# Neighbour broadcast by stream shuffles, and transposes in other places, in a two-layer hybrid decoder trunk

## The chip, the cores and the metric

The kernel runs on one core of a Trainium2 chip. The metric is the device time of one execution in microseconds. PE is the matrix engine, DVE the vector engine, ACT the scalar engine, POOL the general-purpose engine; SP issues most DMAs. Before the change three runs took 1132.7 to 1134.36 us, with a median of 1132.71 us.

## The reference

Input `x` is 1 x 256 x 1024 in float32. There are two layers. Each adds half a SwiGLU feed-forward step, a mixer, and another half step, each on the RMS norm of `x`; a last RMS norm follows. The mixer is what the change is about:

```python
def hybrid_mixer(h, ...):
    proj = h @ w_in                      # 1024 x 7636: all inputs of the branches and the gates
    # a: indexer and sparse attention
    rel   = relu(einsum('bqhd,bsd->bqhs', q_idx, k_idx) * 64 ** -0.5)   # after partial rotary
    score = einsum('bqhs,bqh->bqs', rel, w_idx)
    _, sel = top_k(score, top_k)         # then attention over the selected keys
    # b: forgetting attention
    # c: gated delta rule, chunk 64, on convolved q, k, v (4 heads of 128)
    a_mat = where(strict, einsum('nbhid,nbhjd->nbhij', kb, kc) * decay, 0)
    sol = triangular_solve(a_mat + eye(64), rhs, lower=True, unit_diagonal=True)
    ...
    return (sum_i sigmoid(gate_i) * (y_i @ P_i)) @ w_out

def rms_norm(x, gain):
    return x * rsqrt(mean(x * x) + 1e-6) * gain
```

## The kernel before

**Weights.** All products with weights keep float32 accuracy by splitting both operands into a high and a low part. A weight comes in units of 128 x 2 x 512 (512 KB). SP loads a unit into one of four `raw` buffers; ACT copies it to the reduced type (`hi`) and DVE subtracts (`lo`), into one of three pairs of buffers. PE uses a unit in one of three forms: three products of 512 columns per block of 128 rows (`form_a`, with the tokens as output rows), or with the weight's rows as output (`form_b`), or products of 512 and 256 columns (`form_w`).

**Order.** `Emit` writes the program: while the products of the weight units are emitted, tasks (the branches, normalisations, the merge's halves) are advanced step by step when a modelled clock passes their due time (`E.tick`, `E.run`, `E.finish`). Then a scheduler with a model of the engines sets the order on each engine; splits of weights and evacuations of accumulators have a higher priority. Every engine runs its instructions in that order.

**A mixer** multiplies the normed input with the units of q, k, v of branch c, of the small projection (`sm`), of a's queries, z, b's q and k (`bqk`) and v, then the gates and branches in the order gate 0, gate 1, branch a, gate 2, branch b, branch c, and then `w_out`. Beside these products run the tasks:

- *Branch a* (`branch_a`): POOL rotates `sm` (`rope`) and copies the keys twice (`kdup`); PE transposes (tile `ti`, two tiles of four 128 x 128 transposes); ACT and DVE split the results into `akh`, `akl`, `iqs`. PE multiplies them to scores (`ix`), DVE sums over heads (`score`) and takes the top entries in rounds of MAX8 and MATCH_REPLACE8. The query side of the attention (`qs`) is split in the same way.
- *Branch c* (`branch_c`): of the 128 x 128 triangular matrices it takes the 16 x 16 blocks on the diagonal (`nd`, 8 of each kind in the 8 matrices), packs them into `cp16` (128 x 128) by a reduction, and inverts all by substitution in 15 steps of `ztmp` and `zc` on DVE. Step m needs row m of every block on all 16 partitions of the block. That is the neighbour broadcast: `cp16` is written to a DRAM tile `dr`, and two DMAs read it back into `nb`, each partition of a block getting the block's 16 rows (lines 631 to 635):

```python
dr = dp.tile([P, P], F32, name="dr", tag="dr")
nc.sync.dma_start(dr, cp16)
for i in range(2):
    nc.sync.dma_start(nb[i], bass.AP(tensor=dr.tensor, offset=dr.offset + i * 1024,
                                       ap=[[2048, 8], [0, 16], [1, 1024]]))
```

- *The gates* (`gate`): a product into two accumulator banks, evacuated by DVE with the bias (tile `gate`) and by ACT with tanh. The product after next needs those banks.
- *The merge* (`branch`, `m_half`): DVE multiplies each branch's product by its gate and adds it up in `mrg`. `m_half(n)` transposes half n of it (tile `mt`, 8 transposes) and splits it into pairs `mp` (ACT copies, DVE subtracts). It is a task; `E.finish(mt[u // 2])` completes half 0 ahead of unit 0 of `w_out` and half 1 ahead of unit 2.

**The norm** (`rms`, six times a run: at the start of each half step and mixer): the squares, summed over the feature blocks into `ssum`, are summed over the partitions by products with a column of ones (tile `ss`, 128 x 1, two products), scaled on DVE and raised to the power -1/2 on POOL (`rstd`).

## Time and profile before

| | |
|---|---|
| median of three runs | 1132.71 us |
| the profiled execution | 1133.0 us, of which its span 1131.2 us |
| mean granted PE clock | 0.996 |
| busy: PE, DVE, ACT, POOL | 1108.3, 842.2, 652.2, 198.0 us |
| chain that ended last | PE 91%, DVE 4%, DMA 2%, the rest 1% or less each |
| DMA | 194.07 MB, mean 172 GB/s |

A busy share of 98% says that PE is nearly always at work, and so the list of what stops it is short. Times inside the profile count from the span's start. The mixer of layer 1 begins its tasks near 140 us and ends its merge near 440 us; the second has the same stretches about 557 us later. [...]

### The profile page before, as it was taken

The numbers are of one execution on the slowest core, as the hardware profiler recorded it, in microseconds if no ns is written. First come the engines' busy times: TensorE is split into PE (matmuls) and PEld (weight loads), VectorE is DVE, ScalarE is ACT, GpSimd is POOL, SyncE is SP. The second block draws the span as 40 slices with busy tenths as digits, with TensorE's granted clock in tenths as the row PEclk, the third lists the DMA queues.
The fourth block names the chain that finished last, engine by engine and source line by source line (L and its number), as shares of the span: only waits on it lengthen the run. The fifth ranks groups of instructions, "written<-read, shape, count | busy, mean of one in ns | idle before, by whom it ended". The sixth has DMA issues, their size and how long they took to land.

```text
span 1131.2 us, 17844 instructions
## 1 busy us (share of the span) xinstructions
PE 1108.3 (98%) x6765; PEld 954.2 (84%) x6765; DVE 842.2 (74%) x1373; ACT 652.2 (58%) x1136; POOL 198.0 (18%) x172
## 2 busy tenths in 40 slices
PE   9999999998999999999999999999999999999997
PEld 7888898987778878888888889979877788888886
DVE  7776689879746677876678767888796658787753
ACT  6655455644758645655465645564647685556543
POOL 4322022100000203322032311040000003033210
PEclk9999999999999999999999999999999999999999
DMA  8665655555434354666556555555554344556652
GB/s 285 205 186 189 190 178 184 165 146 167 149 113 144 128 179 154 213 195 188 187 171 202 186 193 182 177 169 168 152 177 150 104 130 147 169 171 200 187 191 91
DMA packets 56375, 194.07 MB, mean 172 GB/s; under 512 B 6240, under 2 KB 8672, under 8 KB 56288
## 3 DMA queue, kind: packets, MB, share of 16 engines
q1 hardware_dynamic: 55856, 192.32, 53.2%
q8 instruction: 53, 0.87, 0.3%
q10 hardware_dynamic: 432, 0.60, 0.1%
q14 instruction: 34, 0.28, 0.1%
HBM read 191.72 MB, written 1.18 MB: 171 GB/s over the span
## 4 chain that ended last, share of the span: by engine, by line
PE 91%; DVE 4%; DMA 2%; issue 1%; POOL 1%; ACT 1%; POOLq 0%; DVEq 0%; ACTq 0%
PE pw L148 48%; PE pt L148 25%; PE pbr L148 6%; PE po L148 4%; DMA nb<-dr 2%; DVE lo L86 1%; PE lg L148 1%; PE pv L148 1%; PE pT L152 1%; PE lv L148 1%; PE lw L148 1%; DVE score L86 1%; PE gq L148 1%; DVE ztmp L86 0%; POOL rp L86 0%
## 5 line engine op out<-in xcount | busy, mean ns | idle before, releaser
L86 DVE TENSOR_TENSOR lo<-raw,hi 128x1024 fp32r<-128x1024 f32 (+2 forms) x353 | 451.2, 1280 | 178.8 <-ACT hi L86 178.2
L86 ACT ACTIVATE hi<-raw 128x1024 fp32r<-128x1024 f32 (+2 forms) x353 | 372.6, 1057 | 353.9 <-PE pw L148 155.7
L148 PE MATMUL pw<-xt,hi 128*128 128x512 f32 x1024 | 349.0, 396 | 0.8 <-ACT hi L86 0.8
L148 PE MATMUL pw<-xt,lo 128*128 128x256 f32 x1024 | 263.8, 280 | 0.0
L148 PEld LDWEIGHTS pw<-xt,hi 128*128 128x128 f32 x1024 | 189.3, 189 | 37.7 <-ACT hi L86 1.7
L148 PE MATMUL pt<-hi,xt 128*128 128x512 f32 (+1 forms) x640 | 206.5, 398 | 4.7 <-DVE gate L86 4.7
L148 PEld LDWEIGHTS pw<-xt,lo 128*128 128x128 f32 x1024 | 193.0, 189 | 9.0 <-DVE lo L86 0.7
L148 PEld LDWEIGHTS pt<-hi,xt 128*128 128x128 f32 x640 | 120.5, 191 | 28.7 <-issue 5.8
L148 PE MATMUL pw<-ht,hi 128*128 128x512 f32 x384 | 132.2, 394 | 0.0
L148 PE MATMUL pt<-lo,xt 128*128 128x512 f32 (+1 forms) x320 | 127.9, 400 | 1.7 <-DVE lo L86 1.7
L148 PE MATMUL pt<-xt,hi 128*128 128x256 f32 x640 | 118.1, 285 | 0.0
L148 PE MATMUL pw<-ht,lo 128*128 128x256 f32 x384 | 103.4, 279 | 0.0
L148 PEld LDWEIGHTS pt<-xt,hi 128*128 128x128 f32 x640 | 99.6, 191 | 0.2
L148 PE MATMUL pt<-xt,lo 128*128 128x256 f32 x320 | 89.7, 284 | 0.0
L148 PEld LDWEIGHTS pw<-ht,hi 128*128 128x128 f32 x384 | 71.4, 188 | 15.2
L86 POOL TENSOR_TENSOR hr<-hg,rbc 128x512 f32<-128x512 f32 x32 | 42.3, 1323 | 213.8 <-DVE hg L86 204.5
L148 PEld LDWEIGHTS pw<-ht,lo 128*128 128x128 f32 x384 | 72.4, 188 | 1.5
L148 PEld LDWEIGHTS pt<-lo,xt 128*128 128x128 f32 x320 | 61.0, 191 | 14.2 <-DVE lo L86 2.6
L86 POOL TENSOR_TENSOR hg<-hr,rbc 128x512 f32<-128x512 f32 x32 | 66.9, 2090 | 2.5
L86 POOL TENSOR_TENSOR ssum<-ssum,sq 128x512 f32<-128x512 f32 x18 | 28.6, 1588 | 199.3 <-ACT sq L86 199.3
L148 PEld LDWEIGHTS pt<-xt,lo 128*128 128x128 f32 x320 | 60.8, 191 | 0.0
L86 POOL TENSOR_TENSOR so<-so,mhalf 128x8 f32<-128x8 f32 x2 | 3.3, 1642 | 284.9 <-DVE so L86 284.9
(254 smaller groups left out, 1498.6 us busy)
## 6 DMA issues: line engine op xcount, KB each, us to landing
raw<-in_wmx SPq DMA_DIRECT2D x112, 512.0 KB, 3.7
raw<-in_wf2i SPq DMA_DIRECT2D x64, 512.0 KB, 3.8
raw<-in_wf1i SPq DMA_DIRECT2D x63, 512.0 KB, 4.2
raw<-in_wf1o SPq DMA_DIRECT2D x32, 512.0 KB, 4.2
raw<-in_wf2o SPq DMA_DIRECT2D x32, 512.0 KB, 4.2
raw<-in_wbr SPq DMA_DIRECT2D x24, 512.0 KB, 3.3
raw<-in_wmo SPq DMA_DIRECT2D x16, 512.0 KB, 4.1
raw<-in_wms SPq DMA_DIRECT2D x8, 468.0 KB, 3.8
```

The costliest lines, as they stand in the source:

```text
L86: return f(*args, **kw)
L148: self.nc.tensor.matmul(out, lhsT, rhs, start=start, stop=stop, skip_group_check=True)
L152: self.nc.tensor.transpose(out, in_, ident)
```

## The change

It has four parts.

1. In `branch_c` the DMAs to and from DRAM go. DVE makes the broadcast with 15 `stream_shuffle` instructions, which pick for each of 32 partitions the partition it reads: in shuffle m all 16 partitions of a block read partition m, and only the columns from m + 1 on are moved.
2. In `rms` the two products with ones become two transposes of 128 x 128, and DVE sums each over the free axis.
3. The index transposes `ti` are pinned by `tc.issue_after(E.pe.ins)`: they are not issued before the last product that has been emitted when the task's step is written.
4. The merge: half 0 is transposed between the two token blocks of the last unit of branch c (`mid`), half 1 ahead of the third row block of `w_out`'s unit 1 (`midway`), both pinned in the same way; the waits by `E.finish` go.

```diff
         return self.parts.pop(self.used - 1)
 
     def mm(self, out, lhsT, rhs, start=True, stop=True, cost=0.218):
-        self.nc.tensor.matmul(out, lhsT, rhs, start=start, stop=stop, skip_group_check=True)
+        self.pe = self.nc.tensor.matmul(out, lhsT, rhs, start=start, stop=stop, skip_group_check=True)
         self.t += cost
 
     def tr(self, out, in_, ident):
-        self.nc.tensor.transpose(out, in_, ident)
+        self.pe = self.nc.tensor.transpose(out, in_, ident)
         self.t += 0.11
 
     def add(self, gen, rank=0, pace=PACE):
...
     rawp = ctx.enter_context(tc.tile_pool(name="rawp", bufs=NR))
     hlp = ctx.enter_context(tc.tile_pool(name="hlp", bufs=NH))
     wk = ctx.enter_context(tc.tile_pool(name="wk", bufs=2))
-    dp = ctx.enter_context(tc.tile_pool(name="dp", bufs=2, space=bass.MemoryType.DRAM))
     ps = ctx.enter_context(tc.tile_pool(name="ps", bufs=4, space=bass.MemoryType.PSUM))
     pa = ctx.enter_context(tc.tile_pool(name="pa", bufs=2, space=bass.MemoryType.PSUM))
     pc = ctx.enter_context(tc.tile_pool(name="pc", bufs=2, space=bass.MemoryType.PSUM))
...
 
     def rms(st):
 
-        pt = pa.tile([P, 512], F32, name="ss", tag="s")
+        pt = pa.tile([P, 2, P], F32, name="ss", tag="s")
         for tb in range(2):
-            E.mm(pt[:, tb:tb + 1], st["sq"][:, tb * P:(tb + 1) * P], ones[:, 0:1], tb == 0, tb == 1, cost=0.11)
+            E.tr(pt[:, tb, :], st["sq"][:, tb * P:(tb + 1) * P], ident)
         r = st["r"] = wk.tile([P, 2], F32, name="rstd", tag="rstd", bufs=2)
-        V.tensor_scalar(r, pt[:, 0:2], 1.0 / D, EPS, op0=OP.mult, op1=OP.add)
+        V.tensor_reduce(r, pt, axis=AX.X, op=OP.add)
+        V.tensor_scalar(r, r, 1.0 / D, EPS, op0=OP.mult, op1=OP.add)
         G.tensor_tensor(out=r, in0=r, in1=mhalf[:, :2], op=OP.pow)
 
     def x_half(nrm, n, st, pt=None):
...
                 E.mm(o, wl[:, i, m0:m0 + P], xk(xt, 0, k), False, b, 0.109)
             E.tick()
 
-    def form_w(pt, xt, ks, wh, wl, first, last):
+    def form_w(pt, xt, ks, wh, wl, first, last, midway=None):
 
 
         for m in range(4):
             m0 = m * P
+            if m == 2 and midway is not None:
+                midway()
             for i in range(UK):
                 k = ks + i
                 E.mm(pt[m], wh[:, i, m0:m0 + P], xt[k // 2][:, k % 2], first and i == 0, False, 0.216)
...
         cp16 = tiny("cp16", P, 1)
         V.tensor_reduce(v3(cp16, 8), nd.rearrange("p (q k r) -> p q r k", q=8, k=8), axis=AX.X, op=OP.add)
         V.tensor_copy(v3(zc, 8), cst[:, None, C_E16:C_E16 + 16].to_broadcast([P, 8, 16]))
-        dr = dp.tile([P, P], F32, name="dr", tag="dr")
-        nc.sync.dma_start(dr, cp16)
-        for i in range(2):
-            nc.sync.dma_start(nb[i], bass.AP(tensor=dr.tensor, offset=dr.offset + i * 1024,
-                                               ap=[[2048, 8], [0, 16], [1, 1024]]))
+
+        nbv = [t.rearrange("p (m q r) -> p m q r", m=8, q=8) for t in nb]
+        for m in range(15):
+            nc.vector.stream_shuffle(nbv[m // 8][:, m % 8, :, m + 1:], v3(cp16, 8)[:, :, m + 1:],
+                                     [16 * (i // 16) + m for i in range(32)])
         yield
         rk = tiny("rk", 8)
         G.tensor_tensor(out=rk, in0=ssk, in1=phalf, op=OP.pow)
...
         tmp = tiny("ztmp", P, 1)
         for m in range(15):
             k = 15 - m
-            V.tensor_tensor(out=v3(tmp, 8)[:, :, :k], in0=nb[m // 8].rearrange("p (m q r) -> p m q r", m=8, q=8)[:, m % 8, :, m + 1:],
+            V.tensor_tensor(out=v3(tmp, 8)[:, :, :k], in0=nbv[m // 8][:, m % 8, :, m + 1:],
                             in1=zv[:, :, m:m + 1].to_broadcast([P, 8, k]), op=OP.mult)
             V.tensor_tensor(out=zv[:, :, m + 1:], in0=zv[:, :, m + 1:], in1=v3(tmp, 8)[:, :, :k], op=OP.subtract)
             if m % 4 == 3:
...
                 V.tensor_tensor(d[other], src[own], d[own].bitcast(F32), op=OP.subtract)
         for tb in range(2):
             pt = pa.tile([P, 4, P], F32, name="ti", tag="s")
-            for i in range(2):
-                E.tr(pt[:, i, :], sm[:, tb, S_IQ + i * P:S_IQ + (i + 1) * P], ident)
-                E.tr(pt[:, 2 + i, :], kdup[:, 256 * tb + 128 * i:256 * tb + 128 * (i + 1)], ident)
+            with tc.issue_after(E.pe.ins):
+                for i in range(2):
+                    E.tr(pt[:, i, :], sm[:, tb, S_IQ + i * P:S_IQ + (i + 1) * P], ident)
+                    E.tr(pt[:, 2 + i, :], kdup[:, 256 * tb + 128 * i:256 * tb + 128 * (i + 1)], ident)
             t0 = tb * P
             S.activation(kh[:, :, t0:t0 + P], pt[:, 2:4, :], AF.Copy)
             V.tensor_tensor(kl[:, :, t0:t0 + P], pt[:, 2:4, :], kh.bitcast(F32)[:, :, t0:t0 + P], op=OP.subtract)
...
                 S.activation(v3(bv, 2)[:, tb, :], pt[tb], AF.Copy, scale=r[:, tb:tb + 1])
         tbb = E.add(branch_b(gd, bqk[0], bqk[1], bv, hh, hl, ta))
         m = wk.tile([P, 2, D], F32, name="mrg", tag="mrg", bufs=1)
-        mt = []
         mp = []
 
         def m_half(n):
-            yield
             for j in range(2):
                 mp.append(pair("mp"))
                 pt = (pa if j else pc).tile([P, 2, T], F32, name="mt", tag="s")
-                for i in range(2):
-                    k = 4 * n + 2 * j + i
-                    for tb in range(2):
-                        E.tr(pt[:, i, tb * P:(tb + 1) * P], m[:, tb, k * P:(k + 1) * P], ident)
+                with tc.issue_after(E.pe.ins):
+                    for i in range(2):
+                        k = 4 * n + 2 * j + i
+                        for tb in range(2):
+                            E.tr(pt[:, i, tb * P:(tb + 1) * P], m[:, tb, k * P:(k + 1) * P], ident)
                 split_pair(mp[-1], pt, 0.5)
 
         gates = [[], [], []]
...
                 pt = banks("pbr")
                 for u in range(2):
                     wh, wl = E.next_unit()
-                    form_a(pt, lambda k: kt(hh, k), lambda k: kt(hl, k), 4 * br + UK * u, wh, wl, UN, u == 0, u == 1)
+                    mid = (br, n, u) == (2, 1, 1)
+                    for tb in range(2):
+                        with tc.issue_after(E.pe.ins) if mid else nullcontext():
+                            form_a(pt, lambda k: kt(hh, k), lambda k: kt(hl, k), 4 * br + UK * u, wh, wl, UN, u == 0, u == 1, (tb,))
+                        if mid and tb == 0:
+                            m_half(0)
                 with tc.high_priority(offset=EOFF):
                     for tb in range(2):
                         mm = m[:, tb, n * 512:(n + 1) * 512]
...
                             tmp = k2("mtmp")
                             V.scalar_tensor_tensor(tmp, ts[n][:, tb, :], 1.0, pt[tb], op0=OP.add, op1=OP.mult)
                             (G if br == 1 else V).tensor_tensor(out=mm, in0=mm, in1=tmp, op=OP.add)
-                if br == 2:
-                    mt.append(E.run(m_half(n)))
 
         for kind, br in SEQ:
             (gate if kind == "g" else branch)(br)
...
             po = wide_banks(n)
             for u in range(4):
                 wh, wl = E.next_unit()
-                E.finish(mt[u // 2])
-                form_w(po, mp, u * UK, wh, wl, u == 0, u == 3)
+                form_w(po, mp, u * UK, wh, wl, u == 0, u == 3, (lambda: m_half(1)) if (n, u) == (0, 1) else None)
             new["tasks"].append(E.run(x_half(nxt, n, new, po)))
         return new
 
```

The instruction counts on PE, ACT and POOL are the same as before. DVE has 36 more (30 shuffles, 6 reductions), SP six DMAs fewer.

**DVE in mixer 1, from the packed blocks to the first step of the substitution** (`cp16` packed blocks, `nb` the broadcast rows, `qs` the queries of branch a, `bqk` the evacuation of b's products, `lo` splits of weight units). Before:

```order
L86 TENSOR_REDUCE cp16_2544<-nd_2538 128x128
L86 TENSOR_TENSOR lo81_2706<-raw81_2512,hi81_2705 128x1024
L86 TENSOR_SCALAR aq_2653<-aq_2653 128x8
L86 TENSOR_TENSOR bqk_2557<-pt_2295,rbc8_1619 128x512
L86 TENSOR_TENSOR bqk_2557<-pt_2296,rbc8_1619 128x512
L86 TENSOR_TENSOR lo82_2762<-raw82_2566,hi82_2761 128x1024
L86 TENSOR_TENSOR qs_2239<-tq_2589,qs_2239 64x4x128
L86 TENSOR_TENSOR qs_2239<-tq_2598,qs_2239 64x4x128
L86 TENSOR_TENSOR ztmp_2803<-nb_2539,zc_2541 128x8x15
L86 TENSOR_TENSOR qs_2240<-tq_2589,qs_2240 64x4x128
```

and now, from the ninth shuffle on (the first eight stand directly ahead, behind `cp16`, a mask of the top-k and `lo81`):

```order
L636 STREAM_SHUFFLE nb_2540<-cp16_2544 128x8x7
L86 TENSOR_TENSOR bqk_2568<-pt_2295,rbc8_1619 128x512
L86 TENSOR_TENSOR bqk_2568<-pt_2296,rbc8_1619 128x512
L636 STREAM_SHUFFLE nb_2540<-cp16_2544 128x8x6
...
L636 STREAM_SHUFFLE nb_2540<-cp16_2544 128x8
L86 TENSOR_TENSOR selb_2597<-selb_2597,cst_107 128x128
L86 TENSOR_TENSOR qs_2239<-tq_2600,qs_2239 64x4x128
L86 TENSOR_TENSOR qs_2239<-tq_2609,qs_2239 64x4x128
L86 TENSOR_SCALAR aq_2664<-aq_2664 128x8
L86 TENSOR_TENSOR ztmp_2814<-nb_2539,zc_2541 128x8x15
L86 TENSOR_TENSOR lo82_2773<-raw82_2577,hi82_2772 128x1024
L86 TENSOR_TENSOR qs_2240<-tq_2600,qs_2240 64x4x128
```

The shuffles stand where the DMA ran, the first step of the substitution waits for nothing off the engine, and `qs_2240` still follows it.

**PE in mixer 1, the index transposes** (`hi65`, `hi70`: the 66th and 71st weight unit). Before, the first of four groups:

```order
L148 MATMUL pt_2048<-hi65_1990,xt_1073 128x512
L148 MATMUL pt_2049<-hi65_1990,xt_1073 128x512
L152 MATMUL ti_2243<-cst_109,sm_2011 128x128
L148 MATMUL pt_2048<-lo65_1991,xt_1073 128x512
L148 MATMUL pt_2048<-hi65_1990,xt_1073 128x512 x2
```

and now:

```order
L148 MATMUL pt_2186<-hi70_2187,xt_1073 128x512
L152 MATMUL ti_2243<-cst_107,sm_2011 128x128
L152 MATMUL ti_2243<-cst_107,kdup_2160 128x128
L152 MATMUL ti_2243<-cst_107,sm_2011 128x128
L152 MATMUL ti_2243<-cst_107,kdup_2160 128x128
L152 MATMUL ti_2254<-cst_107,sm_2011 128x128
L152 MATMUL ti_2254<-cst_107,kdup_2160 128x128
L152 MATMUL ti_2254<-cst_107,sm_2011 128x128
L152 MATMUL ti_2254<-cst_107,kdup_2160 128x128
L148 MATMUL pt_2186<-hi70_2187,xt_1073 128x512
```

The eight transposes are now one block, five units later.

**ACT in the merge of mixer 1** (`hi120` to `hi124`: the first units of `w_out`, of which 120 to 123 make the first half of its output columns and 124 begins the second). Before:

```order
L86 ACTIVATE hi121_4223<-raw121_4123 128x1024
L86 ACTIVATE hi122_4256<-raw122_4149 128x1024
L86 ACTIVATE mp_4198<-mt_4199 128x2x256
L86 ACTIVATE mp_4206<-mt_4207 128x2x256
L86 ACTIVATE mp_4266<-mt_4267 128x2x256
L86 ACTIVATE mp_4274<-mt_4275 128x2x256
L86 ACTIVATE hi123_4294<-raw123_4167 128x1024
```

and now:

```order
L86 ACTIVATE hi121_4218<-raw121_4134 128x1024
L86 ACTIVATE mp_4230<-mt_4231 128x2x256
L86 ACTIVATE mp_4238<-mt_4239 128x2x256
L86 ACTIVATE hi122_4267<-raw122_4160 128x1024
L86 ACTIVATE hi123_4289<-raw123_4178 128x1024
L86 ACTIVATE hi124_4327<-raw124_4204 128x1024
L86 ACTIVATE mp_4303<-mt_4304 128x2x256
L86 ACTIVATE mp_4311<-mt_4312 128x2x256
```

The pairs of half 1 (`mp_4303`, `mp_4311`) now stand behind three more splits, of which the last is that of unit 124, and on PE a block of eight products with unit 124 stands between the transposes of half 1 and the first product with `mp_4303`.

## Rows read from the trace of the kernel before

**Rows 1.** The page: busy time of engines; then the weight splits on DVE and ACT.

```profile
PE 1108.3 (98%) x6765; PEld 954.2 (84%) x6765; DVE 842.2 (74%) x1373; ACT 652.2 (58%) x1136; POOL 198.0 (18%) x172
...
L86 DVE TENSOR_TENSOR lo<-raw,hi 128x1024 fp32r<-128x1024 f32 (+2 forms) x353 | 451.2, 1280 | 178.8 <-ACT hi L86 178.2
L86 ACT ACTIVATE hi<-raw 128x1024 fp32r<-128x1024 f32 (+2 forms) x353 | 372.6, 1057 | 353.9 <-PE pw L148 155.7
```

**Rows 2.** Waits of PE: line, who it waited for, us in total, times, longest.

```profile
PE pt L148 <- DVE gate L86: 4.7, 2, 2.4
PE ix L148 <- DVE qs L86: 2.5, 4, 1.1
PE ti L152 <- POOL sm L86: 2.2, 2, 1.1
PE pt L148 <- DVE lo L86: 1.7, 2, 0.9
```

**Rows 3.** Waits of DVE, the same columns.

```profile
DVE ztmp L86 <- DMA nb<-dr: 9.3, 2, 4.8
```

**Rows 4.** Timeline of DVE in mixer 1: start, us, operation, [idle before, releaser].

```profile
245.80 1.28 DVE L86 TENSOR_TENSOR qs<-tq,qs 64x512 fp32r<-64x512 f32 x2
251.92 0.28 DVE L86 TENSOR_TENSOR ztmp<-nb,zc 128x120 f32<-128x120 f32 x1 [4.84 <-DMA nb<-dr]
...
273.62 1.40 DVE L86 SCALAR_TENSOR_TENSOR gate<-pt,rstd,bg 128x512 f32<-128x512 f32 x2
```

**Rows 5.** Timeline of PE in mixer 1, the same columns.

```profile
253.08 0.36 PE L148 MATMUL ix<-akh,iqs 128*128 128x256 f32 x1 [1.14 <-DVE qs L86]
...
254.12 0.36 PE L148 MATMUL ix<-akh,iqs 128*128 128x256 f32 x1 [0.33 <-DVE qs L86]
...
256.38 0.50 PE L148 MATMUL pt<-lo,xt 128*128 128x512 f32 x1 [0.86 <-DVE lo L86]
...
274.51 0.47 PE L148 MATMUL pt<-hi,xt 128*128 128x512 f32 x1 [2.35 <-DVE gate L86]
```

**Rows 6.** Windows: stretch, us, busy us of PE, PEld, DVE, ACT, POOL, PEclk, DMA share, GB/s.

```profile
275.00:280.00 5.00, 5.00 (x16) 3.95 (x16) 5.00 (x14) 0.67 (x2) 0.00 (x0) 0.66 0.63 236
403.00:408.00 5.00, 3.34 (x22) 2.45 (x21) 5.00 (x8) 3.12 (x5) 0.12 (x1) 1.00 0.66 210
```

**Rows 7.** Timeline of PE, the norm behind mixer 1.

```profile
441.80 0.50 PE L148 MATMUL ss<-cst,ssum 128*128 128x1 f32 x4
442.16 0.48 PE L148 MATMUL pw<-xt,hi 128*128 128x512 f32 x1
...
442.71 0.40 PE L148 MATMUL pw<-xt,hi 128*128 128x512 f32 x1
```

**Rows 8.** Timeline of PE, the merge of mixer 1.

```profile
403.76 1.03 PE L152 MATMUL mt<-cst,mrg 128*128 128x128 f32 x8
405.49 1.39 PE L152 MATMUL mt<-cst,mrg 128*128 128x128 f32 x8 [0.70 <-DVE mrg L86]
407.74 0.50 PE L148 MATMUL pw<-mp,hi 128*128 128x512 f32 x1 [0.86 <-DVE mp L86]
```

**Rows 9.** Tiles `ztmp`, `score`, `X` on DVE: count: duration ns min/median/max, first and last start.

```profile
L86 DVE TENSOR_TENSOR ztmp<-nb,zc x30: 155/219/284, 251.9 to 831.9; 128x120 f32<-128x120 f32 x2, 128x112 f32<-128x112 f32 x2, 128x104 f32<-128x104 f32 x2, 128x96 f32<-128x96 f32 x2
...
L86 DVE MATCH_VALUE_LOAD score<-m,score x32: 67/85/93, 220.1 to 835.2; 128x8 f32 x32
...
L86 DVE STREAM_TRANSPOSE X<-Z x8: 433/553/700, 278.9 to 862.9; 128x512 f32<-128x512 f32 x4, 32x256 f32<-32x256 f32 x4
```

**Rows 10.** Windows of mixer 1 up to the gate, columns as in rows 6.

```profile
190.00:200.00 10.00, 8.92 (x42) 6.73 (x42) 6.79 (x12) 5.02 (x10) 6.27 (x13) 1.00 0.60 196
200.00:213.00 13.00, 13.00 (x63) 10.82 (x62) 10.95 (x28) 7.61 (x13) 4.36 (x12) 1.00 0.53 160
213.00:239.00 26.00, 26.00 (x222) 25.96 (x221) 24.31 (x91) 12.61 (x27) 1.67 (x1) 1.00 0.46 147
239.00:273.00 34.00, 30.83 (x167) 25.68 (x165) 28.00 (x67) 18.83 (x40) 0.00 (x0) 1.00 0.57 167
```

More of the change, by code (lines that the diff above doesn't have):

```diff
@@ L1 @@
-from contextlib import ExitStack
+from contextlib import ExitStack, nullcontext
 import numpy as np
```

## The prediction, as it was put on record

> **What bounds the kernel now.** I read the busy shares first: PE is busy for 1108.3 of 1131.2 us, DVE for 842.2 [rows 1]. Nothing that leaves the amount of PE work alone can therefore bring more than the 22.9 us in which PE stands still, plus what PE loses where its granted clock is low. Then I read who stops PE: in the two mixers it is the gate's evacuation on DVE (4.7 us), the indexer's queries `qs` on DVE (2.5), the rotated small projection `sm` from POOL (2.2) and a weight split `lo` (1.7) [rows 2]. Third came what DVE waits for: the neighbour broadcast `nb`, read back from DRAM, twice, 9.3 us in all [rows 3]. The timelines then show how these hang together. In mixer 1 DVE has its last work before the wait, two of the four `qs`, at 245.80 and stands from 247.1 until 251.92 [rows 4]; the other two `qs` stand behind the first `ztmp` in its queue, so PE's scores `ix` come late (1.14 and 0.33 idle), so does a `lo` (0.86), and DVE gets to the gate's evacuation at 273.62, while PE has stood since 272.16 until 274.51 [rows 4, 5]. [...] Mixer 2 repeats all this: the waits have count 2 [rows 2, 3].
>
> **The sums of squares.** Before, each normalisation puts four short PE passes (two f32 products of one column each) into the stream: they begin at 441.80 and the next product starts 0.36 later and itself takes 0.08 longer than its neighbours, 0.44 in all [rows 7]. Now there are two transposes. Eight transposes in a row take 1.03 us with the tail [rows 8], so about 0.11 each, 0.22 for two. That saves 0.22 x 6 normalisations = **1.3 us**, all on PE. DVE gets six reductions over 128 values and two columns: bounds 0.2 (a `ztmp` of similar size [rows 9]) and 0.7 (the 512-element row of the same group); I take 0.4, 2.4 us spread over the program. The chain to `rstd` gets longer by as much; nothing on PE is listed as waiting for it [rows 2], and I cost it at nothing. If that cover were gone it would be 2.4 us.
>
> **The index transposes.** PE waits 1.1 us at the first one (2.2 for two mixers) because POOL's rotation is not done [rows 2]. The order now shows the eight as one block, behind five further weight units, which is about 10 us later, when the rotation and the copies `kdup` are over; before, they stood in four groups, and each return to products costs some 0.1. Gain per mixer 1.1 + 0.1 for the restart + 3 x 0.1 = **1.5 us**. Below it could be nothing (if the scores needed them at once); above no more than this. The consumers on ACT and DVE move back with it, and DVE's work on the scores starts at about the same time as before; but the convolution work that stood behind the consumers is now done ahead of them.
>
> **The broadcast.** Three DMAs per mixer go from SP's queue; in their place DVE has 15 shuffles of 128x120 down to 128x8. The trace of before has no shuffle. The nearest row is `ztmp`, which has the same 15 shapes: 0.155 to 0.284, median 0.219, so 15 x 0.22 = 3.3 us [rows 9]. The pattern is another for each, and a load of state ahead of an operation costs about 0.09 here (MATCH_VALUE_LOAD [rows 9]); on the other hand independent instructions overlap, which `ztmp` with its dependent partner can't. Lower bound 15 x (0.09 + 0.04) = 2.0 us; upper bound the other stream instruction of this trace, STREAM_TRANSPOSE at up to 0.70, with a state load, 15 x 0.78 = 11.7 us, though it handles 512 elements. I take 3.3, by the row with the same shapes. [...]
>
> What comes of it is decided at one point, the gate's evacuation, because PE leaves it at the later of its own arrival and DVE's arrival plus 0.9 (273.62 to 274.51 [rows 4, 5]). DVE first: between 190 and 273 it is idle for 3.2 + 2.1 + 1.7 + 6.0 = 13.0 us [rows 10], of which the 4.84 of the broadcast goes. The order shows the same work ahead of the gate as before apart from the shuffles, and 6 us more of it (convolution rows) ahead of the first score. So of the other 8.1 idle us some is filled; some stays, as it is waiting for splits on ACT. I take half, 4.0. DVE is then at the gate at 273.6 + 3.3 - 4.8 - 4.0 = 268.1 (bounds 264 and 272.1 by all and none of the 8.1), and PE leaves at 269.0. PE itself would be there at 272.2 - 1.5 (index transposes) - 2.7 (the three pauses before, 2.33, and their restarts) = 268.0: with `qs` no longer behind a DMA these pauses have nothing left that causes them. So PE leaves at 269.0 in place of 274.5, **5.5 us earlier**, with about 1.0 of pause left; the 1.5 of the transposes is inside this and is not added again. A single pause of this size left the clock alone elsewhere: the merge stage has 1.56 us of pauses within 5 us at 1.00 [rows 6, 8]. So the fall after the gate goes too, 1.6. Mixer 1 gains 7.1; mixer 2, whose broadcast wait is 9.3 - 4.84 = 4.5, gains 6.7. Together **13.8 us**. SP is no term: its queue loses six DMAs in all and gains none.
>
> **The merge.** Before, PE makes 16 transposes with a pause of 0.70 for `mrg` and another of 0.86 for the split `mp`, and a restart or two: 2.2 us per mixer besides the transposes [rows 8]. Now the first eight lie inside the last branch unit's products and are covered. The second eight stand with other products behind them, but the order shows ACT's split of the unit after next ahead of `mp`, and that split needs a buffer that PE frees only just before. ACT's two splits (1.06 each) and DVE's `lo` (1.28 each [rows 1]) then have to pass before PE's first two kinds of filler products can start: about 0.8 waiting for `hi` and 0.8 for `lo`, 0.1 for `mrg` and three restarts, 2.0 in all. I take **0.2 per mixer, 0.4 in all**; bounds -0.7 (all splits one further late) and +1.7 (no pause at all but restarts).
>
> **Sum.** 1.3 + 13.8 + 0.4 = 15.5 us. The profiled execution has 1133.0 us, of which 1.8 lie outside its span of 1131.2; the median of the runs shown, 1132.71, is 0.3 below. 1133.0 - 15.5 = **1117.5 us**.
>
> **The rivals.**
> *DVE stays late.* None of the other 8.1 us of idle time is recovered: DVE comes to the gate at 272.1, PE leaves at 273.0, 1.5 earlier, and after longer pauses the clock falls as before. Gain 2 x 1.5 - 0.4 + 1.3 + 0.4 = 4.3, time 1128.7. For it: the waits for splits on ACT are set by buffers, and DVE is busy for all of 275 to 280 [rows 6]. Against it: work that needs no split is moved into those waits by the order. Dearer shuffles at 0.4 (6.0 in all) end half way, at about 1124.
>
> *The clock.* Blocks of eight transposes now stand between products in four new places (index and first merge half of each mixer). If PE's clock fell after them as it does after the gate, each would cost 1.6: 1117.5 + 4 x 1.6 = 1123.9. Against it: 16 transposes among pauses at 403 to 408 ran at 1.00, and so did the products behind [rows 6, 8]. [...]
>
> *Slower.* The shuffles cost what the other stream instruction does: 11.7 us a mixer, 8.4 more than I took. DVE is at the gate at 276.5, PE leaves at 277.4, 2.9 later than before, the clock falls as before: 2 x 2.9 - 1.7 = 4.1 lost, 1137.1. It decides from the point where DVE is later than 273.6 + 0.9 at the gate, that is 6.4 us more than I took or 0.65 us per shuffle. For it: besides the broadcast's wait DVE is idle for 1.2 us only from 239 to the gate [rows 10], so every shuffle's time arrives there. Against it: a shuffle has at most 120 elements.
>
> *Given back.* The gate is passed early, but PE is then held at the next thing DVE or ACT delivers late (second top-k, block inverse, their products), because DVE, full there, has gained less than PE. 5.5 x 2 back and the clock's 3.2 with it: about 1131.5. For it: DVE is busy 5.00 of 5 us in 275 to 280 [rows 6]; against it: at the gate DVE has itself gained the 5.5.
>
> **How the numbers follow.** Forecast 0.62, DVE late 0.17, clock 0.06, given back 0.09, slower 0.06. About 0.2% (2.3 us) can be told from no change, so the first three, 0.85, are faster, given back (1131.5) is same. Low end: DVE no longer binds (PE leaves the gate at its own 268.0, 6.5 earlier: 2 x 8.1 - 0.4 = 15.8), the merge at its bound 3.4, and 1.3: 20.5, so 1112.5. High end: the case of the late DVE, 1128.7. That leaves out the last two cases and little of the others.
>
> **What would show it.** Right: no row of DVE waiting for `nb`; shuffles near 0.2 each; no PE wait for `sm` and next to none for `qs`; the gate's wait at 1 us or less per mixer and the clock at 1.00 after it; PE's wait in the merge moved from `mp` to `hi` and `lo` of a unit; `ss` at 12 passes. Wrong: shuffles over 0.4, a gate wait over 2 us, a clock below 1.00 in 265 to 285, or new waits of PE behind the gate that are not in the list of before.

## The result, and the profile after

| | before | changed |
|---|---|---|
| median of four runs each, us | 1132.7 (1131.66 to 1134.36) | 1120.48 (1120.28 to 1120.72) |
| ratio, 95% interval | | 0.9895 (0.9881 to 0.9909) |
| profiled execution, its span, us | 1133.0, 1131.2 | 1120.34, 1118.4 |
| mean granted PE clock, share of its full rate | 0.996 | 0.999 |

The change makes the kernel 12.2 us faster. The forecast of 1117.5 was 15.2 us below the median of before: right in direction and inside its range, 3.0 us too good. In the three later sets of runs the kernel before had medians of 1131.4 to 1132.0 (25, 7 and 13 runs); against these the changed kernel is 11.0 to 11.5 us faster.

The page of the changed kernel, busy time of the engines: PE has lost 7.3 us against [rows 1], DVE has gained 6.6.

```profile
PE 1101.0 (98%) x6753; PEld 949.8 (85%) x6753; DVE 848.8 (76%) x1439; ACT 651.9 (58%) x1136; POOL 212.7 (19%) x172
```

The waits of PE, columns as in [rows 2]:

```profile
PE pw L148 <- ACT hi L86: 2.7, 4, 1.3
PE pT L152 <- ACT PT L86: 2.0, 2, 1.0
PE pw L148 <- DVE lo L86: 1.7, 3, 0.7
PE pt L148 <- DVE ztmp L86: 1.5, 2, 0.8
PE pt L148 <- DVE bqk L86: 1.3, 2, 0.6
PE spin L237 <- DVE phalf L86: 1.2, 1, 1.2
PE pv L148 <- ACT PT L86: 0.5, 2, 0.3
```

The waits for `qs` and `sm` are gone, and that for `gate` has become 0.8 per mixer (the list puts it down to `ztmp`, which DVE runs between the two halves of the gate's evacuation). Three kinds are new: `hi`/`lo` in the merge, which were forecast; `bqk`, directly behind the shuffles; and `PT`, the transposed attention weights, behind the gate. The last two were not.

The tile `nb` on DVE (columns as in [rows 9]) and the timeline of DVE in mixer 1:

```profile
L636 DVE LOAD_MASK_SELECT nb<-cp x30: 31/36/43, 239.5 to 793.2; - x30
L636 DVE STREAM_SHUFFLE nb<-cp x30: 214/272/343, 239.5 to 793.2; 128x120 f32<-128x120 f32 x2, 128x112 f32<-128x112 f32 x2, 128x104 f32<-128x104 f32 x2, 128x96 f32<-128x96 f32 x2
```

```profile
239.54 0.04 DVE L636 LOAD_MASK_SELECT nb<-cp  x1
239.54 0.32 DVE L636 STREAM_SHUFFLE nb<-cp 128x120 f32<-128x120 f32 x1
239.74 0.04 DVE L636 LOAD_MASK_SELECT nb<-cp  x1
239.74 0.33 DVE L636 STREAM_SHUFFLE nb<-cp 128x112 f32<-128x112 f32 x1
...
241.08 1.30 DVE L86 TENSOR_TENSOR bqk<-pt,rbc 128x512 f32<-128x512 f32 x2
242.28 0.03 DVE L636 LOAD_MASK_SELECT nb<-cp  x1
...
242.90 0.30 DVE L86 TENSOR_TENSOR selb<-selb,cst 128x128 f32<-128x128 f32 x1
...
267.12 0.73 DVE L86 SCALAR_TENSOR_TENSOR gate<-pt,rstd,bg 128x512 f32<-128x512 f32 x1
```

One shuffle takes 0.21 to 0.34, but the next starts 0.20 down to 0.09 later: the fifteen fill 239.54 to 241.08 and 242.28 to 242.90, 2.16 us in all. With each comes a load of its mask, so that DVE has 66 instructions more in the trace (30 shuffles, 30 loads, 6 reductions). The gate's evacuation is at 267.12, against 273.62 in [rows 4], and PE goes on at 268.00, against 274.51 in [rows 5]:

```profile
268.00 0.47 PE L148 MATMUL pt<-hi,xt 128*128 128x512 f32 x1 [0.77 <-DVE ztmp L86]
```

To see where the time came from I compare the two traces by PE's own work: the 5472 products with weights are the same in all kernels here and, but for exchanges between near neighbours, stand in the same order, so the start of the n-th of them is a mark in each. Time between such marks, in us. "Front 1" runs from the 25th product to the product behind the gate of mixer 1, "behind" over the 24 products after it, "back" from there into the feed-forward behind the mixer (its first 64 products), branches and merge with it. "Front 2" begins shortly ahead of mixer 2's wait for `sm` (744.7 us in the kernel before) and ends 16 products behind its gate, where "back 2" begins; "rest" ends at the last product's start.

```
                start  front 1  behind  back 1  between  front 2  back 2   rest
before           12.3    262.2     7.2   160.5    302.5     91.8   164.0  123.9
changed          11.4    256.6     5.6   161.6    301.7     85.2   165.5  124.0
```

Fronts and the clock behind the gate give 5.6 + 1.6 + 6.6 = 13.8 (mixer 2's front holds its own clock fall), start and between 1.7; the backs take 1.1 + 1.5 back. Of the six norms two lie in "between", one in each back and two in front 1. The clock at 275 to 280, columns as in [rows 6], where 0.66 stood:

```profile
275.00:280.00 5.00, 5.00 (x51) 3.83 (x49) 4.31 (x7) 2.32 (x4) 0.00 (x0) 1.00 0.61 187
```

### The profile page after: what moved, and what is told of

Same layout as the page of the kernel before. It is cut to its first block, busy times and chain, and to the rows that moved or that the text cites. A ratio compares the mean times of both kernels' runs of the same rounds, so it can differ in the third digit from the quotient of the medians.

```text
span 1118.4 us, 17866 instructions
## 1 busy us (share of the span) xinstructions
PE 1101.0 (98%) x6753; PEld 949.8 (85%) x6753; DVE 848.8 (76%) x1439; ACT 651.9 (58%) x1136; POOL 212.7 (19%) x172
## 4 chain that ended last, share of the span: by engine, by line
PE 94%; DVE 3%; ACT 1%; issue 1%; DMA 0%; SPq 0%; POOLq 0%; POOL 0%; DVEq 0%
PE pw L148 47%; PE pt L148 28%; PE pbr L148 6%; PE po L148 4%; PE lg L148 2%; DVE lo L86 1%; PE pT L152 1%; PE pv L148 1%; PE lw L148 1%; PE lv L148 1%; PE gq L148 1%; ACT hi L86 0%; DMA xs<-in_x 0%; PE vh L148 0%; PE wv L148 0%
## 5 line engine op out<-in xcount | busy, mean ns | idle before, releaser
L148 PE MATMUL pt<-hi,xt 128*128 128x512 f32 (+1 forms) x640 | 203.9, 393 | 2.8 <-DVE ztmp L86 1.5
```

The source lines that it names most:

```text
L148: self.pe = self.nc.tensor.matmul(out, lhsT, rhs, start=start, stop=stop, skip_group_check=True)
```

## The experiments

**The parts one by one**, each alone on the kernel before: the shuffles (`e1`), the pin of the index transposes (`e2`), the merge (`e3`), the sums of squares (`e4`). Their edits are the parts of the diff above.

> The kernel before with the shuffles alone. Theory (the gate is the tie point: PE leaves it when DVE has evacuated, so only what makes DVE earlier there counts): DVE loses its wait of 4.8 and gets 2.2 us of shuffles, PE keeps its wait for sm, so PE leaves the gate 3 to 5 us earlier per mixer and the half-rate stretch behind it goes (1.6): 8 to 11 us faster, 1122 to 1125. Rival (each wait counts for itself): the waits for qs and lo go (2.7 per mixer) and the gate's wait stays as it was, 5.4 us faster, about 1127, with the half-rate stretch still there.

> The kernel before with the index transposes pinned alone. Theory: PE is 1.5 us earlier per mixer but DVE still waits for the broadcast, so PE waits that much longer for qs or at the gate: within 1 us of before, 1131.7 to 1133.5. Rival (each wait counts for itself): 3.0 us faster, 1129.7.

> The kernel before with the merge's transposes inside neighbouring products alone. Theory: waits of 2.2 us per mixer for mrg and mp become 1.7 for hi and lo of a unit of the second output half: 0.5 to 1.5 us faster, 1131.2 to 1132.2. Rival: the waits are covered and the gain is 3 us or more, below 1129.7.

> The kernel before with the sums of squares by transposes alone. Theory: 24 short passes become 12 transposes, 0.2 us for each of 6 norms: 1.0 to 1.5 us faster, 1131.2 to 1131.7. Rival: the longer chain to rstd is waited for, same or slower.

| | median (range), us | ratio to before, interval |
|---|---|---|
| e1 shuffles | 1126.63 (1125.99 to 1126.84) | 0.9955 (0.9939 to 0.9972) |
| e2 pin | 1128.54 (1126.9 to 1132.74) | 0.9982 (0.9968 to 0.9997) |
| e3 merge | 1130.43 (1127.66 to 1132.39) | 0.9994 (0.9983 to 1.0005) |
| e4 sums of squares | 1128.03 (1125.28 to 1130.12) | 0.9971 (0.996 to 0.9982) |
| before, 25 runs | 1131.44 (1129.08 to 1134.04) | |

```
                start  front 1  behind  back 1  between  front 2  back 2   rest
e1 shuffles      12.1    258.4     5.6   162.1    302.2     86.9   166.7  123.9
e2 pin           11.8    261.6     5.5   160.3    302.2     89.7   164.0  123.9
e3 merge         11.7    262.2     7.2   160.1    302.1     89.3   163.5  124.0
e4 squares       11.6    260.2     5.5   161.6    301.5     88.5   163.6  124.0
```

*e1* has the front's gain (3.8 and 4.9) and the full clock behind the gate, and already the whole loss: its backs are 1.6 and 2.7 longer. It lies at the rival's number, but not for the rival's reason: the wait at the gate did shrink, from 2.4 to 0.8 per mixer, and what it gained was lost behind it. *e3* is as expected, its backs 0.3 and 0.5 shorter; its interval includes no change. *e4*: sixteen products around a norm take 0.22 to 0.24 less for five of the six (none at the program's start), but the whole gain of 3.4 is more than twice what I expected, since the fronts became shorter too. The scheduler, given other durations in the norm, set another order on DVE: the last two `qs` stand together directly behind the first `ztmp`, and PE has no wait at the scores. The broadcast also came back sooner, 8.8 us after the end of `cp16` in mixer 1 in place of 10.6 (mixer 2: 8.6, 10.2); why isn't shown. DVE waits for less of it:

```profile
238.59 1.97 DVE L86 TENSOR_REDUCE cp<-nd 128x128 f32<-128x1024 f32 x1
...
249.35 0.28 DVE L86 TENSOR_TENSOR ztmp<-nb,zc 128x120 f32<-128x120 f32 x1 [2.82 <-DMA nb<-dr]
```

So a part "alone" is never alone here. *e2* shows it as well: PE no longer waits for `sm`, comes to the scores sooner, and waits there, which leaves 0.6 of the 1.5 in front 1. Its median is below both numbers that I had written. Part of that may be the clock: in the profiled execution it did not fall behind the first gate ("behind" 5.5, not 7.2), though PE had paused for 2.3 as before.

```profile
251.90 0.36 PE L148 MATMUL ix<-akh,iqs 128*128 128x256 f32 x1 [2.19 <-DVE qs L86]
```

**The change with one part undone**: the broadcast by DMA again (`e5`), the index transposes without the pin (`e6`).

> The changed kernel with the broadcast through DRAM again, the other three parts kept. Alone the four parts gained 4.8 (shuffles), 2.9 (pin), 1.0 (merge) and 3.4 us (sums of squares). If they add up, this kernel is 7.3 us faster than before and some 4.9 slower than the changed one, about 1124 to 1125. If they share a tie point at the gate, pin and sums of squares gain nothing beyond what DVE allows: 1126 to 1129, with a wait of 2 us or more at the gate in each mixer.

> The changed kernel without the pin of the index transposes. Adding up: 2.9 slower than the changed one, about 1123.4. Tie point: PE loses 1.1 to 2.2 at the transposes per mixer, but 0.8 of it was a wait at the gate anyway: 0.7 to 1.4 per mixer, 1121.9 to 1123.3, and no wait at the gate.

*e5* took 1125.4 us (1124.16 to 1127.3), ratio 0.9944 (0.9927 to 0.9962); *e6* 1127.72 (1126.18 to 1127.86), 0.996 (0.9945 to 0.9976). The shuffles are worth 4.9 in the changed kernel and 4.8 alone: they add up, though e5 lies 0.4 above the range that I had written for that; PE's wait at its gates is 1.5 and 1.7, not 2 or more. The pin is worth 7.2 in it and 2.9 alone (by the interval of e2's ratio 0.3 to 3.6), and neither number that I had written for it held. The waits of PE in e6, and its clock (columns as in [rows 6]) right behind them:

```profile
PE ti L152 <- POOL sm L86: 4.3, 2, 2.1
```

```profile
195.00:200.00 5.00, 5.00 (x19) 3.98 (x18) 2.17 (x4) 1.66 (x3) 1.33 (x5) 0.74 0.44 144
...
747.00:752.00 5.00, 5.00 (x17) 3.88 (x17) 2.36 (x4) 1.58 (x2) 2.74 (x6) 0.66 0.59 206
```

The wait for `sm` has doubled from 1.1 to 2.1 per mixer, and the clock falls behind it in both mixers, to 0.74 and 0.66 over these 5 us. The timeline of POOL in e6 shows where the 1.0 comes from: the first group of the rotation, 2.36 before, takes 3.41 (e4 and e5 have the same 3.42, e1, e2 and e3 have 2.37).

```profile
187.65 3.41 POOL L86 TENSOR_TENSOR rp<-sm,cst 128x48 f32<-128x48 f32 x6 [27.81 <-ACT sm L86]
```

So the pin removes 4.3 of pauses and two falls, together most of the 7.2; the fronts, 3.0 and 3.4 longer than in the changed kernel, hold both (e6 in turn doesn't wait for `bqk`, which costs the changed kernel 1.3).

**How far does DVE's time decide the gate?** Every shuffle is issued twice (`e7`) or four times (`e11`); the result is the same.

```diff
-        for m in range(15):
+        for m in [k for k in range(15) for _ in range(2)]:
```

> The changed kernel with each shuffle issued twice (2.2 us more of DVE per mixer). Tie point: DVE runs without a pause up to the gate, so PE's wait there grows from 0.8 to about 3.0 in each mixer, 4.4 us slower, 1124.9, and 0 to 3 us more where the clock falls after the longer pause. Rival: the second shuffle hides in DVE's slack, less than 1 us slower.

> The changed kernel with each shuffle issued four times (6.5 us more of DVE per mixer). In the order more of the top-k, not less, stands ahead of the gate's evacuation than with two times. Theory: PE's wait at the gate grows from 0.8 to 5 us or more, with the clock falling behind it in some executions: 1128 to 1134. Rival (DVE's slack takes it, as it took the second time): under 1123.

*e7*: 1119.66 us (1119.0 to 1119.79), ratio 0.9891 (0.9876 to 0.9906), so 0.8 less than the changed kernel: the rival held, not the 1124.9 of the tie point. The 2.16 us more of DVE moved the gate's evacuation by only 0.63 (counted from the 25th product), since one round of the top-k (six MAX8 in place of seven) now stands behind it, and the backs were 1.4 and 1.5 shorter. *e11*: 1132.57 (1131.69 to 1133.2), 1.0014 (1.0003 to 1.0026). The 45 further shuffles, an estimated 3 x 2.16 = 6.5 us, made the fronts 8.0 and 7.8 longer than in the changed kernel, but at the scores, not at the gate, and some 3.4 of it is the clock, which falls behind that pause (0.71 and 0.61 in the two windows from 255 to 265 us); the backs are 1.5 and 2.1 shorter.

```profile
PE ix L148 <- DVE qs L86: 6.9, 2, 3.5
```

```profile
255.00:260.00 5.00, 2.31 (x10) 2.04 (x10) 4.84 (x14) 2.11 (x8) 0.00 (x0) 0.71 0.65 208
260.00:265.00 5.00, 5.00 (x22) 4.50 (x21) 5.00 (x19) 2.48 (x9) 0.00 (x0) 0.61 0.26 92
```

With 60 shuffles, an estimated 4 x 2.16 = 8.6 us per mixer or 8.6 / 15 = 0.57 for each of the fifteen, the whole change gains nothing; the rival "slower" had put that point at 0.65. Against the DMA the shuffles lose sooner: e5 has the DMA and the other three parts, and to it e7 (4.3 us of shuffles) is 5.7 faster and e11 7.2 slower. A straight line between the two gives an estimate of 6.2 us per mixer, 0.4 for each of the fifteen; no run lies there.

**What makes the back longer?** Its new waits are for `hi`/`lo` in the merge and for `PT`. ACT in the changed kernel, mixer 1: the scaling of `L` (1.70) stands between two evacuations `PT` of transposed weights, and PE waits for the second and for the tile it frees:

```profile
314.49 0.60 ACT L86 ACTIVATE PT<-pT 128x512 f32<-128x512 f32 x1
314.98 1.70 ACT L86 ACTIVATE L<-L,rsum 128x256 f32<-128x256 f32 x4
316.58 0.58 ACT L86 ACTIVATE PT<-pT 128x512 f32<-128x512 f32 x1
```

```profile
315.14 1.08 PE L148 MATMUL pv<-PT,sm 128*64 128x512 f32 x4 [0.25 <-ACT PT L86]
317.22 0.66 PE L152 MATMUL pT<-cst,L 128*128 128x128 f32 x4 [0.99 <-ACT PT L86]
```

Three edits of the changed kernel, shown shortened and with comments that name the run: `e8` pins the row blocks 2 and 3 of unit 1 of `w_out` behind the transposes of half 1; `e9` issues the scaling of `L` only behind the `PT` copies of the head group before; `e10` writes the shuffles in three pieces of five, so that the scheduler can put other work between them. `e12` has all three.

```diff
+            with tc.issue_after(E.pe.ins) if m >= 2 and midway is not None else nullcontext():   # e8, around the products of form_w
...
+                if scale is not None:            # e9, after transposes(i - 1); scale holds the four activations
+                    with tc.issue_after(E.cp.ins):
+                        scale()
...
+            if m in (4, 9):                      # e10, after each stream_shuffle
+                yield
```

> The changed kernel with the last two row blocks of the unit at the second merge half pinned behind its transposes, so that they and not the next output half's products cover the split. Theory: PE's waits for hi and lo in the merge (1.55 us per mixer besides restarts) go, 2.5 to 3.3 us faster than the changed kernel, about 1117.5. Rival: the splits are late whatever covers them, within 0.7 us of the changed kernel.

> The changed kernel with ACT's scaling of the next group of probabilities written and pinned behind the copies of the transposed ones (PT), in all softmax steps. Theory: what is given back behind the gate is that the second PT copy stands behind four scalings (1.7 us) on ACT, so PE waits 1.0 and 0.25 us for PT in each mixer; with the copies ahead these waits go: 1.5 to 3 us faster than the changed kernel, 1117.5 to 1119. Rival: PE meets the next late thing there (splits, other evacuations), within 0.7 us of 1120.5.

> The changed kernel with the 15 shuffles written in three steps of 5 instead of one. Theory: nine shuffles (1.5 us) stand ahead of the evacuation of b's products, for which PE waits 0.6 us per mixer; in three steps only one stands ahead, and the wait goes, 1 to 1.5 us faster; and the order behind the gate has the PT copies ahead of the scalings, 2 us more: 1117 to 1119.5. Rival: the broadcast is complete later, the substitution and what waits for it come late, same or slower than 1120.5.

> The changed kernel with the pinned cover in the merge, the shuffles in three steps and the scalings behind the copies, all together. If the three waits are separate: 2.2 (measured for the cover) and 2 to 3.3 more, 1115 to 1116.5. If the last two remove the same wait: 1116.5 to 1118.

| | median (range), us | ratio to before, interval |
|---|---|---|
| e8 | 1118.28 (1117.86 to 1118.68) | 0.988 (0.9863 to 0.9897) |
| e9 | 1122.01 (1121.77 to 1122.41) | 0.9915 (0.99 to 0.9931) |
| e10 | 1116.34 (1115.41 to 1116.46) | 0.9863 (0.9847 to 0.9879) |
| e12 | 1113.98 (1113.73 to 1114.26) | 0.9844 (0.9829 to 0.986) |

```
                start  front 1  behind  back 1  between  front 2  back 2   rest
e5 no shuffles   12.5    260.2     5.5   159.8    301.5     90.2   163.2  123.9
e6 no pin        12.1    259.7     5.6   161.5    301.5     88.6   166.2  124.0
e7 double        12.4    257.2     5.6   160.2    301.5     86.2   164.0  124.0
e8 pin of w_out  11.7    256.6     5.6   160.8    301.5     85.3   163.9  124.0
e9 scaling       11.6    256.6     5.5   163.0    301.5     85.2   165.8  123.9
e10 split        12.3    255.5     5.6   160.1    301.5     84.5   164.1  123.9
e11 quadruple    11.6    264.6     5.5   160.2    301.5     93.1   163.4  124.0
e12 all three    11.7    255.9     5.5   159.4    301.5     84.4   162.5  124.0
```

*e8* takes 0.8 and 1.6 out of the backs, somewhat less than forecast: the waits for `hi` and `lo` in the merge fall by 2.6 in all, and 1.5 for `mp` come in. *e9* falls, below both of its numbers: the waits for `PT` are gone, PE waits 1.7 for `yh` (ACT) instead, and the backs are 1.4 and 0.3 longer; the theory that this one wait carries the loss is not borne out. *e10* gains 4.1, more than forecast. In it one shuffle stands ahead of `bqk`, not nine, and PE has no wait there:

```profile
240.15 0.31 DVE L636 STREAM_SHUFFLE nb<-cp 128x120 f32<-128x120 f32 x1
240.33 1.29 DVE L86 TENSOR_TENSOR bqk<-pt,rbc 128x512 f32<-128x512 f32 x2
241.54 0.03 DVE L636 LOAD_MASK_SELECT nb<-cp  x1
```

Its backs are 1.5 and 1.4 shorter as well, without any edit there. *e12* beats both kernels and its forecast: 6.5 us less than the changed one. The gains of e8 and e10 add up to 6.3, so that what e9's edit does in it is not shown; e8 and e10 together without it were not run. PE's waits in e12:

```profile
PE pt L148 <- DVE ztmp L86: 1.7, 2, 0.8
PE pw L148 <- ACT hi L86: 1.5, 2, 0.9
PE pw L148 <- DVE mp L86: 1.4, 2, 0.7
PE spin L237 <- DVE phalf L86: 1.2, 1, 1.2
PE pw L148 <- DVE lo L86: 0.3, 1, 0.3
```

**One order, one time.** The traces allow one comparison more. I take the stretch from 24 products behind a gate to 12 products ahead of the merge, sort the kernels by the order of PE's and ACT's instructions in it, and give its length above that in e5, in us:

| order of PE and ACT | kernels | mixer 1 | mixer 2 |
|---|---|---|---|
| that of the kernel before | before, e2, e3, e4, e5 | 0.00 in all | 0.00 to 0.03 |
| ACT the same, PE nearly | e11 | 0.35 | 0.07 |
| a second | e7, e10 | 0.35, 0.38 | 0.16, 0.21 |
| a third | e1, e6 | 1.81, 1.81 | 2.31, 2.30 |
| a fourth | changed, e8 (mixer 1) | 1.83, 1.82 | 2.24 |
| one of its own | e8 (mixer 2) | | 1.54 |
| one of its own | e9 | 3.27 | 2.61 |
| one of its own | e12 | 0.40 | 0.09 |

Kernels of one order take the same time there to within 0.05 us, although their fronts differ by up to 2.0 us (mixer 1). And e11 keeps the short stretch with four times the shuffles: it is the order that costs the time, not the shuffles in it.

## Why the prediction was right, and where it was off

**Sums of squares, 1.3: right.** `ss` has 12 passes in place of 24, and five norms bring 0.23 each, 1.15. No wait of PE for `rstd` came up.

**The gate, 5.5 + 1.6 and 5.1 + 1.6: right**, measured 5.4 (the 5.6 of the front less its norm) + 1.6 for mixer 1 and 6.6 together for mixer 2. DVE was there at 267.12 (forecast 268.1), PE left at 268.00 (269.0) after a pause of 0.77 (1.0); 0.9 of each difference is the earlier start of this execution ("start" 11.4, not 12.3). The parts inside were less exact. The shuffles took 2.16, not 3.3, near the lower bound of 2.0, which had counted on overlap (its 0.04 per shuffle was my own estimate, which no row shows). A shuffle of 0.32 is followed by the next after 0.20, while in the trace of before the `zc` that needs a `ztmp` of 0.24 starts 0.27 after it (259.88, 260.15); the load of the mask, 0.03 to 0.04, starts together with its shuffle and lies wholly beside the instruction before it. With the broadcast's 4.84 gone, and counted from the 25th product, that leaves 2.9 of DVE's 5.6 us, where the forecast had 4.0 of recovered idle time: the two errors of 1.1 cancel, and that the sum at the gate was met so closely is luck. From 120 elements to 16 the distance from one shuffle's start to the next falls only from 0.20 to 0.09, so in this trace it doesn't go by the elements alone. The pin was priced at 1.5 per mixer by the pauses of [rows 2]; e6 shows it to be worth more than twice that in this kernel, since the pause that it removes had become longer by POOL and the clock fell behind it.

**The clock: right, and less certain than I wrote.** The 1.6 counted for a fall is borne out: in the kernel before the clock stands at 0.50 of its full rate for 3.4 us behind each gate (276.0 to 279.4, 832.4 to 835.8), 1.7 us each, and the 24 products behind the first gate take 7.2 there and 5.6 in the changed kernel. In all four runs of the changed kernel the mean clock is 0.998 or 0.999. But the 3.2 us are a gain only against an execution of the kernel before in which it falls behind both gates, and the same pause is followed by a fall in one kernel and not in another (below). The rival by which the eight transposes in a block pull it down did not come true; here is the stretch behind the index transposes (205.32 to 206.11), columns as in [rows 6]:

```profile
204.00:209.00 5.00, 5.00 (x30) 4.30 (x29) 4.03 (x10) 3.43 (x8) 2.56 (x6) 1.00 0.71 224
209.00:214.00 5.00, 5.00 (x41) 4.81 (x40) 4.67 (x9) 4.71 (x11) 0.00 (x0) 1.00 0.47 133
```

For these eight transposes amid products the trace shows no loss of clock.

**The merge, 0.4: about right**, 0.8 by e3. The pauses moved to `hi` and `lo` as written.

**The step that failed: the sum stopped at the gate.** Behind it the forecast has no term but the gains of merge and norm. By e3 and the norms the backs should have become 0.34 + 0.23 and 0.46 + 0.23 shorter; they became 1.1 and 1.5 longer. So 1.7 and 2.2 are given back, 3.9 in all. The sum by measured terms: 13.6 at the gates, 1.15 for the norms, 0.8 for the merge, 1.2 at the start and in "between" that belong to no part (the start varies from 11.4 to 12.5 among these kernels), less 3.9, is 12.8, the difference of the spans. "Given back" stood only as a rival that takes back everything, because DVE would be full at 275 to 280; what came is a part, and it came in with the shuffles: against e5, which has all but them, the backs are 1.8 and 2.3 longer, and e1, which has only them, shows 1.6 and 2.7. It isn't their time, though, but the order that the scheduler formed with them: e11 has four times as many and gives nearly nothing back. New waits of PE behind the gate were among the prediction's own signs of being wrong, and `PT` is one.

**What stays open** is which instructions of that order cost the time. It isn't that PE arrives there early: e7 arrives 0.6 to 1.0 later than the changed kernel and e10 0.7 to 1.1 sooner, and by the same working give back only 0.2 to 0.8 per mixer. It isn't the wait for `PT` alone (e9). What differs is the order that the scheduler forms from the gate on, and that order turns on small things ahead of it: the same order takes the same time in kernels with different fronts. Which pair of instructions has to change places wasn't isolated.

## What to carry to other kernels

Where one engine is 98% busy and a scheduler fixes the order, price a removed wait by the place where the two engines meet next, and then add a term for the stretch behind it: a few us won at one point come with another order after it. Work that is needed only later should be given to the scheduler in pieces, not in one step; here two places to break, which make three pieces, cost nothing and brought 4.1 us. Value a part by undoing it in the full change as well as by doing it alone: the pin was worth 2.9 us alone and 7.2 with the rest.

## What the runs showed of the hardware that was not expected

**The pause alone doesn't settle whether the clock falls.** Pauses of 2.1 ahead of the index transposes were followed by a fall in both mixers of e6 (0.74 and 0.66 above). e4 has the same two pauses, 2.14 and 2.13, at the same place, and stayed at 1.00 behind both:

```profile
195.00:200.00 5.00, 5.00 (x25) 4.09 (x24) 2.73 (x5) 2.75 (x4) 1.25 (x5) 1.00 0.61 203
...
747.00:752.00 5.00, 5.00 (x24) 4.07 (x23) 3.70 (x6) 1.62 (x3) 2.87 (x6) 1.00 0.71 213
```

e3 paused for 2.35 at the first gate and 2.34 at the second; the clock fell behind the first alone:

```profile
274.00:279.00 5.00, 5.00 (x16) 3.93 (x17) 5.00 (x14) 1.03 (x2) 0.00 (x0) 0.66 0.65 233
829.00:834.00 5.00, 5.00 (x23) 4.10 (x23) 5.00 (x14) 1.48 (x3) 0.00 (x0) 1.00 0.69 226
```

In e4 PE paused for 2.7 at the gate and went on at 1.00:

```profile
268.00:273.00 5.00, 2.34 (x11) 1.66 (x10) 5.00 (x16) 2.32 (x3) 0.00 (x0) 1.00 0.68 188
273.00:278.00 5.00, 5.00 (x23) 4.13 (x22) 5.00 (x14) 1.25 (x2) 0.00 (x0) 1.00 0.51 189
```

In the same execution it fell in the merge behind pauses of 0.71 and 0.86, where in the kernel before it had stayed at 1.00 behind the same two [rows 6, 8]:

```profile
403.00:408.00 5.00, 4.61 (x17) 3.94 (x18) 2.12 (x4) 0.39 (x2) 0.00 (x0) 0.66 0.31 108
```

A fall costs 1.6 to 1.7 us by the 24 products behind the first gate, which take 7.2 with it (before, e3) and 5.5 or 5.6 without. The same kernel also varies: 25 runs of the kernel before spread over 5.0 us (1129.08 to 1134.04, mean clocks 0.994 to 0.998), ten of e4 over 4.8, the four of the changed kernel over 0.44. That the spread narrows with the long pauses fits falls that come in some executions only; four runs against 25 don't show it, and no run was made to.

**The same operations on POOL took one and a half or four times as long.** The six short operations on `sm` that took 2.36 before and 3.41 in e6 take 9.28 in the changed kernel:

```profile
187.30 9.28 POOL L86 TENSOR_TENSOR rp<-sm,cst 128x48 f32<-128x48 f32 x6 [27.81 <-ACT sm L86]
```

The pinned transposes start at 205.32 without a wait, so it costs PE nothing here, but it is what the pin covers. Mixer 2 has the same, 10.80. It isn't the parts of the change as such: e8, which differs in the merge alone, has 3.42 in mixer 1. That the longer group of e6 is real, PE's wait shows, which grew by as much (1.1 to 2.1 per mixer); for the 9.28 and 10.80 no wait of PE does. In mixer 1 of the changed kernel each of the four slow operations of the group (1.75 to 2.58) ends beside a short operation on DVE (0.15 to 0.29), while the other two take 0.3; what slows them wasn't tried.
